# Streaming 16 experts' weights through one core's memory: one more place, single places for two more laps, one expert's gather and sums moved

## The chip, the cores and the metric

One core of a Trainium2 chip runs the whole program. The metric is device time in microseconds (us) of one execution; the time before is the median of three runs, 1548.92 us (1548.19 to 1551.0). Engines are named as in the profile: PE (TensorE) multiplies matrices, PEld is its weight load, DVE (VectorE), ACT (ScalarE) and POOL (GpSimd) work on elements, SP (SyncE) issues the loads from HBM, which 16 DMA engines carry out. The SBUF is the on-chip memory in which all tiles stand, PSUM the small one that PE writes to.

## What is computed

One encoder block on 512 tokens of 1024 numbers, in float32: an RMSNorm, a projection, two attentions (MLA with 16 heads and differential attention with 8), a gated sum with an output projection, and then a mixture of experts, which is the half that the change touches:

```
logits = h @ router_w                       # 16 experts
affinity = softmax(logits)
gate, idx = top_k(affinity per expert, 64)  # each expert picks 64 of the 512 tokens
xe = h[idx]                                 # 16 x 64 x 1024
hidden = silu(xe @ w_gate) * (xe @ w_up)    # w_gate, w_up: 16 x 1024 x 2048
ye = (hidden @ w_down) * gate               # w_down: 16 x 2048 x 1024
out = x + scatter_add(ye at idx)
```

## The kernel before

The first part, to about 600 us, is the attention and the output projection; the routing (the top 64 tokens of each expert) follows and ends at about 627 us. The rest is the experts, one after the other, and all their weights pass through the SBUF once: 402 MB.

**Chunks.** The weights are cut into 384 chunks of [128, 2048] float32, 1 MB each, 24 an expert: 8 for the gate product, 8 for the up product, 8 for the down product. PE uses them strictly in that order. In this text chunk 0 is the first one; expert 1 uses chunks 24 to 47, expert 2 chunks 48 to 71 and so on. The generator `chunks` (L719) yields a chunk at each `next(stream)` and issues its load on SP's queue; the loads stand on that queue in the order of the chunks (a manual dependency from each to the next), so a load that waits for its place holds up all behind it.

**Places.** A chunk stands in a place of 8 KB a partition, named by a letter and a number. E has 4 places, A 5 and, after the first laps, H 4 and B 6 (`REGION`, L32). In the first laps, H and B are not there yet: their memory is held by four single tiles h (the buffers that held the output projection's operand) and six single tiles b, which lie over the tiles of the output projection and the routing. Further there are two places m, one x and one c that are used at the start and then serve other tiles (m: the sums `acc`, x: the hidden layer `hh`, c: `yo`, which takes an expert's outputs).

**Laps.** `FIRST` (L34), `SECOND` (L37) and `LAP` (L41) list the places in the order in which chunks go into them, as (letter, first place, number of chunks in one load). FIRST puts 23 chunks one by one. SECOND puts 21 more chunks: m, m, A4, E one by one, A in two loads of two, then b2, h, b one by one; and then a lap of 16 chunks in loads of two over E, A, H and B. All later laps go over 16 places (4 each of E, A, H, B) in loads of four. `loads` (L702) chains the lists; the last 16 chunks are cut into loads of two and one.

When chunk 44 is used (L1016, in expert 1's down product), the tiles h and b are closed and H and B are opened over the same memory. The first load into H is a new tile over four h places, and the first into B one over all b places.

**Experts.** Two experts make a pair. `gather(pr)` (L929) picks a pair's 128 tokens: DVE makes a one-hot tile `oh` (L902) and a scaled one `ohr` (L932), PE multiplies them with the tokens `xm` (L949, 64 instructions a pair) and DVE moves the product to `xeT` (L951). Pair 0's gather runs piece by piece beside expert 0's gate product. For every later pair it runs in the middle of the pair before: after the second expert's hidden layer is transposed (L1005) and before its down product (L1011). `combine(pr)` (L907) adds a pair's outputs to the sums: the one-hot tile times the affinities, its transpose `ohT` (L914), and eight products (L920) that DVE adds to `acc` (L923). It is a generator, and one step of it is taken beside each chunk of the next expert's gate and up products (L984).

In an expert, the gate and up products are L988, the product of both is L1000, its transpose L1005, the down product L1025. `oh` and `ohr` have a pool of their own, mo2 (L683).

The code is written against a layer that places instructions on the engines' queues; `tc.issue_after(ins)` puts what is traced in its block, on the engine of `ins`, behind `ins`.

Of the kernel before, what the change touches and what calls it, by code (L numbers as in the profile page):

```python
# [11 lines left out]
F32 = mybir.dt.float32  # L12
# [9 lines left out]
T, D, NT, KT = 512, 1024, 4, 8  # L22
# [6 lines left out]
NE, CAP, FF = 16, 64, 2048  # L29


REGION = {"E": 4, "A": 5, "H": 4, "B": 6}  # L32

FIRST = [("m", 0, 1), ("m", 0, 1), ("A", 4, 1)] + [("E", i, 1) for i in range(4)] + [("x", 0, 1)]  # L34
FIRST += [("A", i, 1) for i in range(4)] + [("b", 2, 1)] + [("h", 0, 1)] * 4
FIRST += [("b", i, 1) for i in (0, 1, 3, 4, 5)] + [("c", 0, 1)]
SECOND = [("m", 0, 1), ("m", 0, 1), ("A", 4, 1)] + [("E", i, 1) for i in range(4)] + [("A", 0, 2), ("A", 2, 2)]  # L37
SECOND += [("b", 2, 1)] + [("h", 0, 1)] * 4 + [("b", i, 1) for i in (0, 1, 3, 4, 5)]

SECOND += [(r, i, 2) for r in "EAHB" for i in (0, 2)]  # L40
LAP = [(r, 0, 4) for r in "EAHB"]  # L41

LAST = 16
NPR = NE // 2
# [12 lines left out]
def build(tc, A, out):  # L57
    nc = tc.nc
    V, S, G, PE, SY = nc.vector, nc.scalar, nc.gpsimd, nc.tensor, nc.sync
# [39 lines left out]
    with ExitStack() as es:  # L99
# [60 lines left out]
        for n in range(2):  # L160
            p = ps_tile("s", "anb")
# [6 lines left out]
        for t in range(NT):  # L168
            j = p0p.tile([128, D], F32, name="junk", tag="junk", bufs=2)
# [7 lines left out]
            for n in range(2):  # L177
                xs = xt[t][:, n * 512:(n + 1) * 512]
                V.scalar_tensor_tensor(xs, xs, rx, anb[n], OP.mult, OP.mult)
                p = ps_tile("tr", "xT")  # L180
# [71 lines left out]
        r = small("r", [128, NT, 16])  # L252
# [52 lines left out]
        for t in range(NT):  # L305
            for a, (c0, c1) in enumerate(((0, 256), (256, 544))):
                p = ps_tile("pj", "zcp")[:, :c1 - c0]
                proj3(p, [h_sta(k, t) for k in range(KT)],
                      [(wc[k // 2][:, 0, k % 2, c0:c1], wc[k // 2][:, 1, k % 2, c0:c1]) for k in range(KT)])
                j = pap.tile([128, 256], F32, name="junk", tag="sq", bufs=2)  # L310
# [15 lines left out]
        for a in range(4):  # L326
            p = ps_tile("tr", "cT")
# [139 lines left out]
        for g in range(4):  # L467
            if g < 3:
                grp[g + 1] = None
            for pair in range(2):  # L470
                q, kn, kv = grp[g]
                c = 2 * g + pair
# [7 lines left out]
                p = ps_tile("tr", "rsT")  # L480
# [3 lines left out]
                p = ps_tile("pv", "pv")  # L484
# [180 lines left out]
        lap1 = ExitStack()  # L665
# [14 lines left out]
        ringE = es.enter_context(tc.tile_pool(name="ringE", bufs=1, side="right", reuse_waits="tile"))  # L680
        mo = es.enter_context(tc.tile_pool(name="moe", bufs=1, side="right", reuse_waits="tile"))
        ringA = es.enter_context(tc.tile_pool(name="ringA", bufs=1, side="right", reuse_waits="tile"))
        mo2 = es.enter_context(tc.tile_pool(name="moe2", bufs=1, side="right", reuse_waits="tile"))  # L683
        ew = A["expert_w"]
        pools = {"m": (lambda: mpool, "m8", 2), "c": (lambda: ringC, "wc", 1), "x": (lambda: ringX, "wx", 1),
                 "E": (lambda: ringE, "we", 1), "A": (lambda: ringA, "wa", 1), "B": (lambda: ringB, "wb", 1),
# [14 lines left out]

        def loads():  # L702
            todo = 3 * KT * NE
            for r, i, n in chain(FIRST, SECOND, LAP * NE * 3):
                if todo <= LAST and n == 4:
                    for j in (0, 2):
                        if todo > 2:
                            yield r, j, 2
                        else:
                            yield r, 2, 1  # L710
                            yield r, 3, 1
                        todo -= 2
                    if not todo:
                        return
                    continue
                todo -= n
                yield r, i, n
# [32 lines left out]
        for c0, c1 in ((0, 2), (2, 4), (4, 6), (6, 7), (7, 8)):  # L750
            for t in range(NT):
                hi, lo = mt_[t][:, 0, c0:c1], mt_[t][:, 1, c0:c1]
                m = mrgs[c0 // 4][:, c0 % 4:(c1 - 1) % 4 + 1, t * 128:(t + 1) * 128]
# [70 lines left out]
        for n in range(2):  # L824
# [15 lines left out]
            for t in range(NT):  # L840
                xT = wpool.tile([128, KT, 128], F32, name="xT", tag="wr", bufs=2)
                xm_part(t, 0, 4, xT, S)
                p = ps_tile("pj" if t else "s", "wo")
# [34 lines left out]
        for t in range(NT - 1):  # L878
            n = NT - 1 - t
            PE.matmul(pr_[:, :, t + 1:], on_b, mk[:, :, t, None, :].to_broadcast([128, 2, n, NE]),  # L880
                      start=False, stop=False)
        for t in range(NT):
            PE.matmul(pr_[:, 1], on_b, mk[:, 0, t, None, :].to_broadcast([128, NT, NE]),
                      start=False, stop=t == NT - 1)
# [14 lines left out]
        out_rows = out2.rearrange("t (a c) -> (t a) c", a=2)  # L899

        def one_hot(pr):
            oh = mo2.tile([128, NT, 2, CAP], F32, name="oh", tag="oh", bufs=1)  # L902
            V.tensor_tensor(oh, io[:, None, None, :].to_broadcast([128, NT, 2, CAP]),
                            slot[:, :, 2 * pr:2 * pr + 2, None].to_broadcast([128, NT, 2, CAP]), OP.is_equal)
            return oh
# [23 lines left out]
        def gather(pr):  # L929


            ohr = mo2.tile([128, NT, 2, CAP], F32, name="ohr", tag="ohr", bufs=1)  # L932
            if pr == 0:
                for t in range(NT):
                    for a in range(2):
                        V.tensor_scalar(ohr[:, t, a], io, slot[:, t, a:a + 1], rrs[:, t:t + 1],  # L936
                                        op0=OP.is_equal, op1=OP.mult)
            else:
                oh = one_hot(pr)
                V.tensor_tensor(ohr, oh, rrs[:, :, None, None].to_broadcast([128, NT, 2, CAP]), OP.mult)  # L940
            xT = mo.tile([128, KT, 128], F32, name="xeT", tag="xeT", bufs=1)
            got[pr] = xT, None, None
            n = 1 if pr == 0 else 4
            for k0 in range(0, KT, n):
                p = mps.tile([128, n, 128], F32, name="xeTp", tag="tr", bufs=2)
                for k in range(n):
                    kk = k0 + k
                    for t in range(NT):
                        PE.matmul(p[:, k], xm[:, t, kk * 128:(kk + 1) * 128],  # L949
                                  ohr[:, t].rearrange("p a s -> p (a s)"), start=t == 0, stop=t == NT - 1)  # L950
                V.tensor_tensor(xT[:, k0:k0 + n], p,  # L951
                                vT[:, FN + k0:FN + k0 + n, None].to_broadcast([128, n, 128]), OP.mult)
                yield
            if pr < NPR - 1:
                return
            sidx = mo.tile([128, 2], I32, name="sidx")
            gate = mo.tile([128, 2], F32, name="gate")
            got[pr] = xT, sidx, gate
            p = mps.tile([128, 4], F32, name="sg", tag="tr", bufs=2)
            for a in range(2):  # L960
                for hf in range(2):
                    for t in range(NT):
                        PE.matmul(p[hf * 64:(hf + 1) * 64, 2 * a:2 * a + 2], oh[:, t, a], tg[:, t, 2 * pr + a],
                                  start=t == 0, stop=t == NT - 1)
            pp = p.rearrange("p (a b) -> p a b", b=2)
            V.tensor_scalar(sidx, pp[:, :, 0], 2.0, half, op0=OP.mult, op1=OP.add)
            V.tensor_copy(gate, pp[:, :, 1])
            yield

        got = {}  # L970
        comb = iter(())
        first = gather(0)
        next(first)
        for e in range(NE):
            pr, par_ = divmod(e, 2)
            if par_ == 0:
                cur, sidx, gate = got[pr]
            gu = []
            for up in range(2):
                pp = [mps.tile([128, 512], F32, name="gu", tag="gu", bufs=5) for _ in range(2)]  # L980
                for k in range(KT):
                    if e == 0 and not up:
                        next(first, None)
                    next(comb, None)  # L984
                    wt = next(stream)
                    for j in range(2):
                        for hf in range(2):
                            PE.matmul(pp[j][hf * 64:(hf + 1) * 64], cur[:, k, par_ * 64:(par_ + 1) * 64],  # L988
                                      wt[:, hf * 1024 + j * 512:hf * 1024 + (j + 1) * 512],
                                      start=k == 0, stop=k == KT - 1)  # L990
                gu.append(pp)
                if not up:
                    if e == 0:
                        hh = ringX.tile([128, 2, 1024], F32, name="hh", tag="wx", bufs=1)
                    hid, hT = hh[:, 0], hh[:, 1].rearrange("p (k q) -> p k q", k=8)
                    for j in range(2):
                        S.activation(hid[:, j * 512:(j + 1) * 512], pp[j], AF.Silu)  # L997
# [3 lines left out]
            for j in range(2):  # L1001
                p = mps.tile([128, 512], F32, name="hTp", tag="tr", bufs=2)
# [5 lines left out]
                    S.activation(dst, p, AF.Copy)  # L1008
                else:
                    V.tensor_copy(dst, p)  # L1010
            if par_ == 1 and pr + 1 < NPR:  # L1011
                for _ in gather(pr + 1):
                    pass
            y = mps.tile([128, 512], F32, name="y", tag="y", bufs=1)
            for i in range(8):
                if e == 1 and i == 4:  # L1016
                    lap1.close()
                    ringH = es.enter_context(tc.tile_pool(name="ringH", bufs=1, reuse_waits="tile"))
                    ringB = es.enter_context(tc.tile_pool(name="ringB", bufs=1, reuse_waits="tile"))
                wt = next(stream)  # L1020
                for j in range(2):
                    kt = 2 * i + j
                    hf, f = divmod(kt, 8)
                    for a in range(2):
                        PE.matmul(y[a * 64:(a + 1) * 64], hT[:, f, hf * 64:(hf + 1) * 64],  # L1025
                                  wt[:, j, a * 512:(a + 1) * 512], start=kt == 0, stop=kt == 15)
            if pr == NPR - 1:
                ys = mo.tile([128, 512], F32, name="ys", tag="ys", bufs=1)
                V.tensor_scalar(ys, y, gate[:, par_:par_ + 1], None, op0=OP.mult)
# [44 lines left out]
```

## Time and profile before

| | us |
|---|---|
| median of three runs | 1548.92 |
| the profiled execution | 1547.91 |
| its span, first to last instruction | 1546.2 |
| PE busy | 1418.1 |
| DVE busy | 565.3 |
| ACT busy | 376.8 |
| POOL busy | 157.1 |

The span lacks 1.7 us of the execution's own time, which lie around it. PE was granted 0.979 of its full clock over the span. 441.57 MB were read from HBM, 402 of them weights of the experts. The busy times are shares of the whole; the two halves of the kernel have different limits, so the stretches of the trace are read one by one. In the trace's rows a tile's name stands before the arrow and what it is made of behind it: `wA<-in_expert_w_dram` is a load into A, `gu<-wA,xeT` a gate or up product with a chunk that stands in A. A chunk is 8 matrix instructions of PE, so x32 is four chunks.

### The profile page before, as it was taken

What the parts mean: (1) busy time and instruction counts of PE and PEld (TensorE: products, weight loads), DVE (VectorE), ACT (ScalarE), POOL (GpSimd) and SP (SyncE); (2) the same over time, 40 slices, a digit from 0 to 9 for tenths busy, and PEclk for the clock granted to TensorE, in tenths of its full rate; (3) what the DMA queues carried; (4) which work ended last, traced back from release to release, by engine and by line L of the source; (5) the groups of instructions that cost most, each with busy time, mean ns of one, the idle gap of its engine ahead of it and who ended that gap; (6) DMA issues with size and microseconds to landing.
All of it is one profiled execution on the core that took longest, in us unless ns stands there. A gap on an engine that the chain in (4) does not pass through costs nothing. (4 is left out here: it accounts for less than half of the span.)

```text
span 1546.2 us, 17925 instructions
## 1 busy us (share of the span) xinstructions
PE 1418.1 (92%) x7119; PEld 794.1 (51%) x7119; DVE 565.3 (37%) x1412; ACT 376.8 (24%) x830; POOL 157.1 (10%) x213
## 2 busy tenths in 40 slices
PE   7999999999999898799999979989989979979977
PEld 6777767788888676434334324324324324325322
DVE  8966646548888886301102102002102002102100
ACT  4545555536566643000000000000000000000000
POOL 3003213023434410000000000000000000000000
PEclk9999999999999999899999999999999999999989
DMA  4412113132222259898999999999999999999997
GB/s 158 129 53 62 58 42 105 38 92 59 76 54 54 70 193 373 306 422 370 414 433 430 432 431 431 431 433 433 432 433 433 430 432 433 432 434 432 428 421 283
DMA packets 73718, 448.50 MB, mean 290 GB/s; under 512 B 5765, under 2 KB 47809, under 8 KB 56098
## 3 DMA queue, kind: packets, MB, share of 16 engines
q1 hardware_dynamic: 72192, 444.29, 70.2%
q0 software_dynamic: 1440, 3.07, 0.8%
q8 instruction: 56, 0.92, 0.2%
q14 instruction: 28, 0.23, 0.0%
q10 hardware_dynamic: 2, 0.00, 0.0%
HBM read 441.57 MB, written 5.77 MB: 289 GB/s over the span
## 5 line engine op out<-in xcount | busy, mean ns | idle before, releaser
L1000 DVE TENSOR_TENSOR hh<-hh,gu 128x512 f32<-128x512 f32 x32 | 22.0, 688 | 428.9 <-PE gu L988 428.9
L988 PE MATMUL gu<-wA,xeT 128*64 128x512 f32 x528 | 120.7, 609 | 14.0 <-DMA wA<-in_expert_w_dram 14.0
L988 PE MATMUL gu<-wE,xeT 128*64 128x512 f32 x512 | 115.3, 601 | 11.6 <-DMA wE<-in_expert_w_dram 11.6
L988 PE MATMUL gu<-wB,xeT 128*64 128x512 f32 x448 | 103.6, 617 | 15.3 <-DMA wB<-in_expert_w_dram 15.3
L988 PE MATMUL gu<-wH,xeT 128*64 128x512 f32 x448 | 104.1, 618 | 12.4 <-DMA wH<-in_expert_w_dram 12.4
L997 ACT ACTIVATE hh<-gu 128x512 f32<-128x512 f32 x32 | 19.0, 597 | 345.6 <-PE gu L988 345.6
L211 PE MATMUL dqkv<-hl,hTh 128*128 128x384 f32 x256 | 88.4, 346 | 0.3 <-DVE hl L527 0.3
L988 PEld LDWEIGHTS gu<-wA,xeT 128*64 128x64 f32 x528 | 40.3, 140 | 91.9 <-issue 89.4
L210 PE MATMUL dqkv<-hl,hTh 128*128 128x384 f32 x256 | 87.2, 341 | 0.0
L927 POOL DMA_DIRECT2D out_dram<-acc x4 | 2.2, 558 | 824.8 <-DVE acc L923 824.8
L212 PE MATMUL dqkv<-hl,hTl 128*128 128x384 f32 x256 | 85.5, 338 | 0.0
L988 PEld LDWEIGHTS gu<-wE,xeT 128*64 128x64 f32 x512 | 36.3, 138 | 86.0 <-issue 68.2
L988 PEld LDWEIGHTS gu<-wB,xeT 128*64 128x64 f32 x448 | 32.8, 142 | 84.8 <-issue 63.9
L1008 ACT ACTIVATE hh<-hTp 128x512 f32<-128x512 f32 x16 | 9.6, 597 | 272.1 <-PE hTp L1005 272.1
L988 PEld LDWEIGHTS gu<-wH,xeT 128*64 128x64 f32 x448 | 32.1, 142 | 83.5 <-issue 64.3
L949 PEld LDWEIGHTS xeTp<-ohr,xm 128*128 128x128 f32 x512 | 59.8, 196 | 7.6 <-issue 6.3
L949 PE MATMUL xeTp<-ohr,xm 128*128 128x128 f32 x512 | 62.5, 282 | 1.3 <-DVE ohr L936 1.3
L1025 PE MATMUL y<-wH,hh 128*64 128x512 f32 x224 | 52.2, 621 | 10.9 <-DMA wH<-in_expert_w_dram 10.9
L920 PE MATMUL comb<-yo 128*128 128x512 f32 x112 | 55.5, 622 | 5.7 <-ACT yo L1037 2.8
L1038 DVE COPY yo<-y 64x512 f32<-64x512 f32 x14 | 9.7, 694 | 139.0 <-ACT yo L1037 138.9
L1025 PE MATMUL y<-wE,hh 128*64 128x512 f32 x256 | 56.5, 594 | 1.2 <-DMA wE<-in_expert_w_dram 1.2
L581 POOL TENSOR_SCALAR bias<-dist 128x512 f32<-128x512 f32 x32 | 50.0, 1569 | 48.4 <-DVE st L589 31.6
(366 smaller groups left out, 2600.0 us busy)
## 6 DMA issues: line engine op xcount, KB each, us to landing
wE<-in_expert_w_dram SPq DMA_DIRECT2D x20, 4096.0 KB, 29.1
wA<-in_expert_w_dram SPq DMA_DIRECT2D x19, 4096.0 KB, 29.7
wH<-in_expert_w_dram SPq DMA_DIRECT2D x19, 4096.0 KB, 30.1
wB<-in_expert_w_dram SPq DMA_DIRECT2D x19, 4096.0 KB, 26.5
wr<-in_w_in_dram SPq DMA_DIRECT2D x64, 192.0 KB, 2.6
wb<-in_expert_w_dram SPq DMA_DIRECT2D x12, 1024.0 KB, 12.9
wA<-in_expert_w_dram SPq DMA_DIRECT2D x6, 2048.0 KB, 13.4
wE<-in_expert_w_dram SPq DMA_DIRECT2D x9, 1024.0 KB, 7.1
```

Source lines behind the costliest of these rows:

```text
L210: PE.matmul(p, sh, mh, start=first and k == 0, stop=False)
L211: PE.matmul(p, sh, ml, start=False, stop=False)
L212: PE.matmul(p, sl, mh, start=False, stop=last and k == n - 1)
L581: G.tensor_scalar(bias, dist[:, t], slope, None, op0=OP.mult)
L920: PE.matmul(p, ohT[:, t * 128:(t + 1) * 128], ysp[:, n], start=True, stop=True)
L949: PE.matmul(p[:, k], xm[:, t, kk * 128:(kk + 1) * 128], ohr[:, t].rearrange("p a s -> p (a s)"), start=t == 0, stop=t == NT - 1)
L988: PE.matmul(pp[j][hf * 64:(hf + 1) * 64], cur[:, k, par_ * 64:(par_ + 1) * 64], wt[:, hf * 1024 + j * 512:hf * 1024 + (j + 1) * 512], star ...
L997: S.activation(hid[:, j * 512:(j + 1) * 512], pp[j], AF.Silu)
L1000: V.tensor_tensor(hs, hs, gu[1][j], OP.mult)
L1008: S.activation(dst, p, AF.Copy)
L1025: PE.matmul(y[a * 64:(a + 1) * 64], hT[:, f, hf * 64:(hf + 1) * 64], wt[:, j, a * 512:(a + 1) * 512], start=kt == 0, stop=kt == 15)
L1038: V.tensor_copy(ysp[own, 1], y[64:])
```

## The change

- There is a seventh b place, b6, and FIRST ends with it: 24 places, 24 chunks one by one. To make room, the pool mo2 goes: `oh` moves into the last 512 columns of `yo`, and `ohr` into the slot of `ys` in the pool mo.
- SECOND is replaced by MORE, 60 chunks long: a lap of 22 chunks (m, m, A4, E singly, A as 1, 2, 1, then b2, h and b singly), one of 18 (E and A in loads of two, A4, b2, h and four b singly) and one of 20 (the same with six b). Loads of four over 16 places begin with chunk 84 instead of 60.
- H and B are opened when chunk 84 is used, in the middle of expert 3's up product, instead of at chunk 44.
- The gather of pair 1 is no longer ahead of expert 1's down product but behind it. The later gathers stay where they were.
- The sums of pair 0 are no longer taken one step beside each chunk of expert 2 from its first on, but two steps beside each chunk of its up product. The later sums stay where they were.

```diff
-REGION = {"E": 4, "A": 5, "H": 4, "B": 6}
+REGION = {"E": 4, "A": 5, "H": 4, "B": 7}
...
-FIRST += [("b", i, 1) for i in (0, 1, 3, 4, 5)] + [("c", 0, 1)]
-SECOND = [("m", 0, 1), ("m", 0, 1), ("A", 4, 1)] + [("E", i, 1) for i in range(4)] + [("A", 0, 2), ("A", 2, 2)]
-SECOND += [("b", 2, 1)] + [("h", 0, 1)] * 4 + [("b", i, 1) for i in (0, 1, 3, 4, 5)]
-
-SECOND += [(r, i, 2) for r in "EAHB" for i in (0, 2)]
+FIRST += [("b", i, 1) for i in (0, 1, 3, 4, 5)] + [("c", 0, 1), ("b", 6, 1)]
+SINGLE = [("b", 2, 1)] + [("h", 0, 1)] * 4 + [("b", i, 1) for i in (0, 1, 3, 4, 5, 6)]
+MORE = [("m", 0, 1), ("m", 0, 1), ("A", 4, 1)] + [("E", i, 1) for i in range(4)]
+MORE += [("A", 0, 1), ("A", 1, 2), ("A", 3, 1)] + SINGLE
+MORE += [(r, i, 2) for r in "EA" for i in (0, 2)] + [("A", 4, 1)] + SINGLE[:-2]
+MORE += [(r, i, 2) for r in "EA" for i in (0, 2)] + [("A", 4, 1)] + SINGLE
...
-            for r, i, n in chain(FIRST, SECOND, LAP * NE * 3):
+            for r, i, n in chain(FIRST, MORE, LAP * NE * 3):
...
-            oh = mo2.tile([128, NT, 2, CAP], F32, name="oh", tag="oh", bufs=1)
+            oh = yo[:, 1536:].rearrange("p (t a s) -> p t a s", t=NT, a=2)
...
-            ohr = mo2.tile([128, NT, 2, CAP], F32, name="ohr", tag="ohr", bufs=1)
+            ohr = mo.tile([128, NT, 2, CAP], F32, name="ohr", tag="ys", bufs=1)
...
-                    next(comb, None)
+                    if e != 2:
+                        next(comb, None)
+                    elif up:
+                        with tc.issue_after(mm.ins):
+                            next(comb, None)
+                            next(comb, None)
+                    if e == 3 and up and k == 4:
+                        lap1.close()
+                        ringH = es.enter_context(tc.tile_pool(name="ringH", bufs=1, reuse_waits="tile"))
+                        ringB = es.enter_context(tc.tile_pool(name="ringB", bufs=1, reuse_waits="tile"))
...
-            if par_ == 1 and pr + 1 < NPR:
+            if par_ == 1 and 1 < pr + 1 < NPR:
                 for _ in gather(pr + 1):
                     pass
...
-                if e == 1 and i == 4:
-                    lap1.close()
-                    ringH = es.enter_context(tc.tile_pool(name="ringH", bufs=1, reuse_waits="tile"))
-                    ringB = es.enter_context(tc.tile_pool(name="ringB", bufs=1, reuse_waits="tile"))
...
+            if e == 1:
+                with tc.issue_after(mm.ins):
+                    for _ in gather(1):
+                        pass
```

In the products, `mm` is now the name of the last matrix instruction; the instructions are the same.

## Rows read from the trace of the kernel before

**Rows 1.** The page, part 2: GB/s moved in 40 slices of 38.7 us.

```profile
GB/s 158 129 53 62 58 42 105 38 92 59 76 54 54 70 193 373 306 422 370 414 433 430 432 431 431 431 433 433 432 433 433 430 432 433 432 434 432 428 421 283
```

**Rows 2.** Stretches: us, each engine busy (instructions), granted clock, DMA share, GB/s.

```profile
630.00:635.00 5.00, 5.00 (x27) 2.90 (x28) 0.87 (x3) 0.00 (x0) 0.00 (x0) 0.89 0.18 28
635.00:656.00 21.00, 21.00 (x112) 9.38 (x110) 3.44 (x8) 1.09 (x2) 0.00 (x0) 1.00 0.93 344
656.00:661.00 5.00, 5.00 (x26) 1.62 (x24) 0.00 (x0) 0.00 (x0) 0.00 (x0) 1.00 0.82 298
...
722.00:728.00 6.00, 6.00 (x32) 2.16 (x30) 2.14 (x4) 0.60 (x1) 0.00 (x0) 1.00 0.32 93
745.00:750.00 5.00, 5.00 (x20) 1.59 (x18) 1.37 (x2) 0.00 (x0) 0.00 (x0) 1.00 0.84 308
900.00:1400.00 500.00, 445.64 (x2046) 166.88 (x2042) 58.67 (x87) 22.62 (x38) 0.00 (x0) 0.98 1.00 432
...
661.00:720.00 59.00, 58.59 (x308) 25.03 (x306) 6.03 (x9) 2.98 (x5) 0.00 (x0) 1.00 1.01 427
```

**Rows 3.** Timeline of SP's queue: start us, us, engine, line, what is issued.

```profile
613.03 0.44 SPq L732 DMA_DIRECT2D wc<-in_expert_w_dram  x1
633.22 3.28 SPq L732 DMA_DIRECT2D wm<-in_expert_w_dram  x2
...
650.95 0.33 SPq L732 DMA_DIRECT2D wE<-in_expert_w_dram  x1
...
656.10 3.76 SPq L732 DMA_DIRECT2D wA<-in_expert_w_dram  x2
...
659.53 0.33 SPq L732 DMA_DIRECT2D wA<-in_expert_w_dram  x1
...
725.17 0.81 SPq L732 DMA_DIRECT2D wB<-in_expert_w_dram  x2
...
746.63 0.33 SPq L732 DMA_DIRECT2D wA<-in_expert_w_dram  x1
```

**Rows 4.** Timeline of PE in experts 0 to 3, where chunks, gather and sums stand.

```profile
652.46 7.04 PE L988 MATMUL gu<-wA,xeT 128*64 128x512 f32 x32
...
710.70 7.41 PE L949 MATMUL xeTp<-ohr,xm 128*128 128x128 f32 x64
718.04 7.09 PE L1025 MATMUL y<-wb,hh 128*64 128x512 f32 x32
...
733.42 3.03 PE L920 MATMUL comb<-yo 128*128 128x512 f32 x6 [0.69 <-ACT yo L1037]
...
742.93 3.65 PE L988 MATMUL gu<-wA,xeT 128*64 128x512 f32 x16
746.51 1.98 PE L920 MATMUL comb<-yo 128*128 128x512 f32 x4
...
798.83 7.09 PE L988 MATMUL gu<-wA,xeT 128*64 128x512 f32 x32 [0.43 <-DMA wA<-in_expert_w_dram]
808.40 8.78 PE L988 MATMUL gu<-wH,xeT 128*64 128x512 f32 x32 [2.48 <-DMA wH<-in_expert_w_dram]
```

**Rows 5.** Timeline of DVE, the last reader of the scratch tile sc.

```profile
623.83 0.28 DVE L854 MAX8 top<-sc 16x8 f32<-16x128 f32 x1
```

**Rows 6.** Loads issued at 613, 651, 656 and 660 us: KB each, us to landing.

```profile
wc<-in_expert_w_dram SPq DMA_DIRECT2D x1, 1024.0 KB, 17.3
...
wE<-in_expert_w_dram SPq DMA_DIRECT2D x1, 1024.0 KB, 5.6
...
wA<-in_expert_w_dram SPq DMA_DIRECT2D x1, 2048.0 KB, 7.3
...
wA<-in_expert_w_dram SPq DMA_DIRECT2D x1, 2048.0 KB, 8.8
```

**Rows 7.** Waits of PE for loads from 640 to 860 us: total, times, longest.

```profile
PE gu L988 <- DMA wH<-in_expert_w_dram: 2.5, 1, 2.5
...
PE gu L988 <- DMA wA<-in_expert_w_dram: 0.4, 1, 0.4
```

More of the change, by code (lines that the diff above doesn't have):

```diff
@@ L682, in build @@
         ringA = es.enter_context(tc.tile_pool(name="ringA", bufs=1, side="right", reuse_waits="tile"))
-        mo2 = es.enter_context(tc.tile_pool(name="moe2", bufs=1, side="right", reuse_waits="tile"))
         ew = A["expert_w"]
@@ L987, in build @@
                         for hf in range(2):
-                            PE.matmul(pp[j][hf * 64:(hf + 1) * 64], cur[:, k, par_ * 64:(par_ + 1) * 64],
-                                      wt[:, hf * 1024 + j * 512:hf * 1024 + (j + 1) * 512],
-                                      start=k == 0, stop=k == KT - 1)
+                            mm = PE.matmul(pp[j][hf * 64:(hf + 1) * 64], cur[:, k, par_ * 64:(par_ + 1) * 64],
+                                           wt[:, hf * 1024 + j * 512:hf * 1024 + (j + 1) * 512],
+                                           start=k == 0, stop=k == KT - 1)
                 gu.append(pp)
@@ L1024, in build @@
                     for a in range(2):
-                        PE.matmul(y[a * 64:(a + 1) * 64], hT[:, f, hf * 64:(hf + 1) * 64],
-                                  wt[:, j, a * 512:(a + 1) * 512], start=kt == 0, stop=kt == 15)
+                        mm = PE.matmul(y[a * 64:(a + 1) * 64], hT[:, f, hf * 64:(hf + 1) * 64],
+                                       wt[:, j, a * 512:(a + 1) * 512], start=kt == 0, stop=kt == 15)
+            if e == 1:
+                with tc.issue_after(mm.ins):
+                    for _ in gather(1):
+                        pass
             if pr == NPR - 1:
```

## The prediction, made before the changed kernel was run

> **What bounds the kernel now.** The kernel has two halves, and the first thing to read is the page's row of GB/s in 40 slices [rows 1]: up to slice 14 it mostly moves some tens of GB/s, from slice 21 to slice 39 it stands at 421 to 434. The second half is the 16 experts, 384 chunks of 1 MB of weights, and it runs at the speed of the loads. A view by stretches confirms it [rows 2]: from 900 to 1400 us the loads move 432 GB/s, while PE is busy 445.64 of 500 us, so 54 us of it are idle. At 432 GB/s a chunk of 1.0486 MB takes 2.43 us. Such a stage ends when the last chunk has landed, and nothing makes that earlier but time in which the loads stood still. So I read the same view where the rate is below 432, and count what each stretch lost as its length times (1 - rate/432): 4.7 us in 630 to 635 (28 GB/s), 4.3 in 635 to 656 (344), 1.6 in 656 to 661 (298), 0.7 in 661 to 720 (427), 4.7 in 722 to 728 (93), 1.4 in 745 to 750 (308). That is 17 us, and PE is busy through all of these: here the loads wait for places that PE still reads.
>
> The queue's rows say which place each hole waits for [rows 3]. All 23 places are asked for by 613.03; the next load, into the first m, goes out only at 633.22, when PE has used chunk 0. Up to 651 the loads then follow PE at 2.95 us a chunk (two issues of 0.33 span 3.28), since PE does a piece of the first gather beside each chunk. At 656.10 a load of two chunks into A goes out, which needs chunks 8 and 9. At 725.17 the first load into B goes out. It brings two chunks and needs only b0 and b1 for that, but it begins a new tile over all six b places, and 725.17 is the end of chunk 43 (b5), the last of the four that PE does from 718.04 [rows 4]. At 746.63 the first load of four into A goes out, as chunk 51 ends (742.93 + 3.65). Both places come back late because they come back in blocks, and PE has just done 7.41 us of gather (710.70) and does 8.0 us of sums in three pieces (3.03, 3.03, 1.98) from 733.42 on [rows 4].
>
> **The 24th place** (the last entry of FIRST). Place b6 lies over the scratch tile sc of the routing, whose last reader ends at 624.1 [rows 5]. The load of chunk 23 can go out then, behind the load into c (613.03, landing 17.3 us later [rows 6], 630.3), and lands at about 632.7, in time in which nothing moved. The m load still waits for 633.22, but brings chunk 24 instead of 23: from there on every place brings a later chunk. Worth one chunk, 2.4 us; nothing, if b6 comes free only after 633.
>
> **A in pieces of 1, 2 and 1** (MORE). PE does the four A chunks from 652.46 at 1.72 us each (7.04 less an overlap of some 0.17, over 4) [rows 4], so A0 is free at 654.4 and not, with A1, at 656.1. The load before it is issued at 650.95 and lands 5.6 us later [rows 3, 6], at 656.6, so the engines then hardly run empty. A1 and A2 follow at 657.8; a load of two that met an empty queue took 7.3 us [rows 6], which gives 665.1, and three chunks at 2.43 after 656.6 give 663.9. I take 665.0 for chunk 33, near the slower end. Before, chunk 33 landed at 659.53 + 8.8 = 668.3 [rows 3, 6]. By here 3.3 us are gained, 2.4 by the 24th place and 0.9 by this piece (between 0 and the 1.6 that 656 to 661 lost).
>
> **Singles and pairs up to chunk 84** take the two block waits away. Before, the block of chunks 80 to 83 landed at 798.8, where PE's wait for it ends [rows 4]. From chunk 33 that is 130.5 us for 50 chunks, where 50 x 2.427 is 121.4: 9.1 lost. 6.1 of it are the holes at 722 and 745, the rest the slow start after each. In return 34 of the 50 chunks come singly, at the 427 GB/s of 661 to 720, where most loads are singles [rows 2]: 2.456 us each, 34 x 0.03 = 1.0. Chunk 83 lands at 665.0 + 121.4 + 1.0 = 787.4, 11.4 us earlier.
>
> **Does a new wait come instead?** I follow PE through the new order with the old durations [rows 4]. Expert 1 ends its up half as before; its down half starts where the gather started, 710.70, and takes 8 x 1.72, to 724.5. The gather follows to 731.9, the gate half of expert 2 to 745.6, its up half with 8.0 us of sums and 0.7 of transposes to 768. The loads of chunks 64 and 65 need chunks 46 and 47 (724.5) and are wanted when chunk 63 is about to land, 665 + 30 x 2.45 = 738.5. Chunks 66 and 67 need 49 (735.4), wanted at 743.4. 70 and 71 need 53 (742.3), wanted at 753. The first block of four, 84 to 87, needs 67 (about 777), wanted at 787. The block into B now needs all seven b places, the last with chunk 83 (about 804), and brings 96 to 99, wanted at 816. Everywhere 8 us or more are left; a load wants about 1 of them between issue and first byte.
>
> **The gather and the sums behind.** Their PE time is the same, 7.41 and 8.0 us, only later. Were neither moved, chunk 49 would end at 740.0, where the first two thirds of expert 2's sums are still ahead [rows 4], and chunk 53 at some 752, against wanted times of 743 and 753. So for the loads I cost the moves at nothing; they give margin. What covers them on PE is the stock of loaded chunks: from 640 to 860 PE waits for loads 0.4 and 2.5 us [rows 7]. The gather's evacuation now stands directly ahead of the gate half, but only its second part, under 1 us, and four steps of the gate half cover that. The one-hot tile moves into the free end of yo and ohr into the slot of ys; both had one buffer and have one. SP issues some 20 more loads of 0.33 us on a queue that mostly waits. Nothing, each; if a cover is gone, it comes out of the 8 us of margin.
>
> **The sum** is 3.3 + 9.1 - 1.0 = 11.4 us. All later loads shift by as much: from 900 us on there is no hole to absorb it, and PE, with 54 idle us in 500, can follow. The profiled execution took 1547.91 us (its span is 1546.2), which would become 1536.5. The median of the runs is 1.0 higher, 1548.92, so I forecast 1537.5.
>
> **Rivals.** *Part of it is lost*: b6 comes free late (2.4 less, 1540), or PE reaches expert 2 later than I count, so that a hole stays (4 to 6 less, 1541.5 to 1543.5). For it: a margin of 8 us is no more than one gather. Against it: every duration is from the row of the same instruction. 19 in 100.
>
> *Slower: the single loads run one at a time.* From 635 to 656 us singles go out 2.95 us apart and move 344 GB/s, 3.05 us a chunk [rows 2, 3]. That happens when each place comes free less than one transfer ahead. If it held for the 24 chunks that are newly single (44 and 45, ten of 54 to 63, twelve of 72 to 83), they would cost 24 x (3.05 - 2.43) = 14.9 us, more than what is gained: 1548.9 - 12.4 + 14.9 = 1551.4 (12.4 is the sum without its 1.0 for singles). It decides from 20 such chunks on. The Trainium skill, page "DMA: Bandwidth & Descriptors", section "Bandwidth", speaks for this one: it has 341 GB/s for a load of 1 MB by itself and 425 for 16 MB, and advises large loads; by its figures the 24 chunks would cost an estimated 24 x 0.61 = 14.6 us. The trace agrees with that from 635 to 656, where loads come alone. Against it: from 661 to 720 singles are queued ahead of the engines, and 427 GB/s are moved; by the margins above the new ones are queued ahead as well. 6 in 100.
>
> *No change*: with 16 places from chunk 84 on, the loads wait later for what they gained early, and it ends at 1549. That needs PE to fall 16 chunks behind in experts 4 and 5; its idle time speaks against it. 6 in 100.
>
> **How the numbers follow.** My own case has 69 in 100: 1535 to 1540, with 0 to 2.4 for the 24th place, 0 to 1.6 for the A piece and 6.1 to 9.1 for the block waits. The range of 1534.5 to 1543.0 takes in most of the partial case and leaves out some 15 in 100. About 0.2%, 3 us, is what a measurement of this kernel can tell from no change. Faster by more than that, below 1545.8, are my case and the partial one, 0.88. The same 0.06, slower 0.06.
>
> **What would show it.** In the profile after: a load into b6 at about 624, and nothing moving for some 1.7 us before 634 instead of 4; a load into A at 654.4; no stretch under 420 GB/s from 665 to 900; in expert 1 the down half and then the gather, and the sums in the up half of expert 2; the first block of four landing near 797, where PE now waits for its chunks until 808.4 [rows 4]. I am wrong if the rate shows a hole between 730 and 860, if singles queued ahead move under 400 GB/s, or if the holes are gone and the end is not earlier by the same time.

## Result and profile after

The changed kernel takes 1538.76 us (median of four runs, 1537.32 to 1539.41), beside 1548.99 us for the kernel before (1548.19 to 1551.0): a ratio of 0.9931, with a 95% interval of 0.9914 to 0.9948. That is 10.2 us, where 11.4 were forecast. The profiled execution took 1537.32 us, its span is 1535.6. All medians here are of executions at the usual clock: one slow execution of the kernel with 23 places (1606.57 us, granted clock 0.846) and one of the kernel before (1791.11 us, 0.748) are left out.

The page's row of GB/s in 40 slices (here of 38.4 us) answers to [rows 1]. In the kernel before, slices 17 to 20 read 306, 422, 370 and 414; now they read 345, 404, 428 and 428:

```profile
GB/s 159 129 54 63 58 43 105 38 90 63 75 50 59 65 196 355 345 404 428 428 432 434 434 431 431 435 431 432 431 432 434 431 432 436 427 432 435 428 421 278
```

The stretches of the changed kernel (us, busy time of PE, PEld, DVE, ACT and POOL with instructions, granted clock, DMA share, GB/s) answer to [rows 2]:

```profile
629.00:634.00 5.00, 5.00 (x24) 2.18 (x25) 0.58 (x2) 0.00 (x0) 0.00 (x0) 0.82 0.24 59
634.00:655.00 21.00, 21.00 (x112) 9.35 (x110) 1.46 (x5) 1.09 (x2) 0.00 (x0) 1.00 0.96 348
655.00:660.00 5.00, 5.00 (x26) 1.71 (x24) 0.00 (x0) 0.00 (x0) 0.00 (x0) 1.00 0.92 333
660.00:665.00 5.00, 5.00 (x26) 1.45 (x22) 0.56 (x1) 0.00 (x0) 0.00 (x0) 1.00 0.98 418
665.00:720.00 55.00, 54.59 (x260) 19.68 (x260) 6.86 (x11) 2.98 (x5) 0.00 (x0) 1.00 1.01 428
720.00:740.00 20.00, 20.00 (x126) 11.53 (x124) 2.08 (x3) 0.59 (x1) 0.00 (x0) 1.00 1.02 432
740.00:760.00 20.00, 20.00 (x76) 6.37 (x72) 7.25 (x11) 1.77 (x3) 0.00 (x0) 1.00 1.00 423
760.00:900.00 140.00, 135.53 (x644) 50.49 (x644) 18.32 (x28) 6.54 (x11) 0.00 (x0) 1.00 1.01 433
900.00:1400.00 500.00, 447.77 (x2100) 173.31 (x2097) 61.25 (x91) 23.22 (x39) 0.00 (x0) 0.98 1.00 432
```

The holes at 722 and 745 (93 and 308 GB/s before) are gone: 432 and 423. The stretch beside the first gather, 634 to 655, moves what it moved before (348 GB/s, 344 before). Ahead of the first m load there is still a hole. The same eight microseconds of both kernels, the kernel before first, then the changed one:

```profile
628.00:636.00 8.00, 8.00 (x40) 5.05 (x39) 2.32 (x8) 0.00 (x0) 0.00 (x0) 0.81 0.32 105
...
628.00:636.00 8.00, 8.00 (x41) 4.25 (x40) 0.88 (x3) 0.00 (x0) 0.00 (x0) 0.82 0.52 191
```

That is 8 x (1 - 105/432) = 6.1 us lost before and 4.5 after. The prediction's sign was 4 and then 1.7: both sizes were too small by 2 us or more. The hole is shorter by 1.6 us: a chunk, 2.4 us, less the 0.8 by which the m load of this execution came later after the load into c (632.04 - 611.05 = 20.99 us, where it was 633.22 - 613.03 = 20.19 [rows 3]).

The timeline of SP's queue in the changed kernel (start us, us, engine, line, operation), which answers to [rows 3]:

```profile
611.05 0.44 SPq L733 DMA_DIRECT2D wc<-in_expert_w_dram  x1
622.16 0.33 SPq L733 DMA_DIRECT2D wb<-in_expert_w_dram  x1
632.04 3.28 SPq L733 DMA_DIRECT2D wm<-in_expert_w_dram  x2
...
653.21 0.33 SPq L733 DMA_DIRECT2D wA<-in_expert_w_dram  x1
...
656.64 0.33 SPq L733 DMA_DIRECT2D wA<-in_expert_w_dram  x1
```

And that of PE at the end of expert 1, which answers to the second part of [rows 4]:

```profile
709.57 10.52 PE L1031 MATMUL y<-wb,hh 128*64 128x512 f32 x48
...
723.46 7.41 PE L950 MATMUL xeTp<-ohr,xm 128*128 128x128 f32 x64
730.80 3.65 PE L998 MATMUL gu<-wE,xeT 128*64 128x512 f32 x16
```

The load into b6 goes out at 622.16, right as the last reader of sc ends, the load into A0 at 653.21 by itself (the one into A1 and A2 follows at 656.64), and the gather stands behind the down product. All of this is as the prediction drew it, only some 1.2 us earlier: the first m is reloaded at 632.04, not 633.22.

**A yardstick for all runs.** That shift belongs to the first half of the program, which the runs hardly touch (it gains the load into b6) and which ends at another moment in each execution: the first m load went out between 632.04 and 636.16 us over the profiles of this study. From there on the loads set the pace. So I compare the runs by the span less the start of that load, and call it the second half. Each is read from one profile. It was 1546.2 - 633.22 = 913.0 us before and 1535.6 - 632.04 = 903.6 us after, 9.4 less. A second profile of the changed kernel, with a load at 635.09 and a span of 1538.5, has 903.4.

### The profile page after: what moved, and what is told of

Its sections match the earlier page's. It is cut to its first block, busy times and chain, and to the rows that moved or that the text cites. A ratio compares the mean times of both kernels' runs of the same rounds, so it can differ in the third digit from the quotient of the medians.

```text
span 1535.6 us, 17967 instructions
## 1 busy us (share of the span) xinstructions
PE 1414.2 (92%) x7119; PEld 792.8 (52%) x7119; DVE 564.6 (37%) x1412; ACT 376.9 (25%) x830; POOL 156.7 (10%) x213
## 5 line engine op out<-in xcount | busy, mean ns | idle before, releaser
L998 PE MATMUL gu<-wA,xeT 128*64 128x512 f32 x512 | 114.9, 601 | 9.8 <-DMA wA<-in_expert_w_dram 9.8
L998 PE MATMUL gu<-wH,xeT 128*64 128x512 f32 x384 | 86.4, 604 | 14.7 <-DMA wH<-in_expert_w_dram 14.7
L998 PE MATMUL gu<-wB,xeT 128*64 128x512 f32 x384 | 88.1, 613 | 11.6 <-DMA wB<-in_expert_w_dram 11.6
L998 PEld LDWEIGHTS gu<-wA,xeT 128*64 128x64 f32 x512 | 36.6, 138 | 85.3 <-issue 70.1
L998 PEld LDWEIGHTS gu<-wB,xeT 128*64 128x64 f32 x384 | 29.4, 141 | 69.5 <-issue 66.3
L998 PEld LDWEIGHTS gu<-wH,xeT 128*64 128x64 f32 x384 | 27.4, 139 | 72.7 <-issue 52.4
L1031 PE MATMUL y<-wA,hh 128*64 128x512 f32 x256 | 57.1, 595 | 1.2 <-DMA wA<-in_expert_w_dram 1.2
L1047 ACT ACTIVATE yo<-y 64x512 f32<-64x512 f32 x14 | 8.2, 589 | 196.8 <-PE y L1031 196.8
```

Source lines behind the costliest of these rows:

```text
L998: mm = PE.matmul(pp[j][hf * 64:(hf + 1) * 64], cur[:, k, par_ * 64:(par_ + 1) * 64], wt[:, hf * 1024 + j * 512:hf * 1024 + (j + 1) * 512], ...
L1031: mm = PE.matmul(y[a * 64:(a + 1) * 64], hT[:, f, hf * 64:(hf + 1) * 64], wt[:, j, a * 512:(a + 1) * 512], start=kt == 0, stop=kt == 15)
L1047: S.activation(ysp[own, 0], y[:64], AF.Copy)
```

## The experiments

Ten runs were made, nine kernels and the changed one once more. The table has for each the median of its runs, the ratio to the kernel before, run on the same chip, with its 95% interval, and the second half of its profile.

| kernel | median us | ratio [interval] | first m load, span | second half |
|---|---|---|---|---|
| before | 1548.99 | 1 | 633.22, 1546.2 | 913.0 |
| changed | 1538.76 | 0.9931 [0.9914, 0.9948] | 632.04, 1535.6 | 903.6 |
| changed, again | 1538.99 | 0.9937 [0.9923, 0.9950] | 635.09, 1538.5 | 903.4 |
| both moves alone | 1543.70 | 0.9962 [0.9949, 0.9975] | 636.16, 1544.5 | 908.3 |
| gather's move alone | 1545.68 | 0.9983 [0.9974, 0.9993] | 633.31, 1543.9 | 910.6 |
| sums' move alone | 1546.16 | 0.9982 [0.9973, 0.9991] | 634.28, 1545.5 | 911.2 |
| 24th place alone | 1549.10 | 0.9999 [0.9991, 1.0008] | 634.77, 1548.1 | 913.3 |
| changed, moves undone | 1539.76 | 0.9936 [0.9923, 0.9949] | 635.15, 1538.4 | 903.3 |
| changed, 23 places | 1540.40 | 0.9947 [0.9932, 0.9962] | 633.09, 1539.3 | 906.2 |
| changed, 120 more singles | 1543.65 | 0.9966 [0.9953, 0.9978] | 634.16, 1541.9 | 907.7 |
| gate and up in turn | 1536.80 | 0.9924 [0.9910, 0.9939] | 632.82, 1535.0 | 902.2 |
| the same, A singly | 1536.53 | 0.9925 [0.9911, 0.9938] | 632.13, 1534.0 | 901.9 |

### The changed kernel with both moves undone

```diff
-                    if e != 2:
-                        next(comb, None)
-                    elif up:
-                        with tc.issue_after(mm.ins):
-                            next(comb, None)
-                            next(comb, None)
+                    next(comb, None)
...
-            if par_ == 1 and 1 < pr + 1 < NPR:
+            if par_ == 1 and pr + 1 < NPR:
...
-            if e == 1:
-                with tc.issue_after(mm.ins):
-                    for _ in gather(1):
-                        pass
```

Expected:

> The changed kernel with both moves taken back: 24 places, single places to chunk 84, gather and sums where they were. The prediction: the moves are only margin, no hole opens, 1538 to 1540 us (changed kernel: 1538.8). Its tightest places are the loads into A2 and A3 that need chunk 53, with 0.3 us left. Rival: the margins are too thin, holes of 2 to 5 us open between 740 and 755, 1541 to 1544.

Measured: 1539.76 us, and a second half of 903.3, that of the changed kernel. Its stretches where a hole was to be feared:

```profile
720.00:740.00 20.00, 20.00 (x90) 6.71 (x89) 4.85 (x7) 1.19 (x2) 0.00 (x0) 1.00 1.02 429
740.00:760.00 20.00, 20.00 (x79) 6.32 (x80) 4.82 (x7) 1.19 (x2) 0.00 (x0) 1.00 1.00 425
```

No hole opens, though PE does gather and sums as early as it did before. In the changed kernel the two moves are margin that nothing uses, as the prediction had it; the places alone do it.

### The two moves without the places

The edit is the same one the other way round, on the kernel before.

> The kernel before with the two moves alone (pair 1's gather behind expert 1's down product, pair 0's sums in expert 2's up half); 23 places and the block laps as before. Theory A, the block waits are set by when PE ends chunk 43 and chunk 51: with the gather behind, chunk 43 ends near 717.7 us and not at 725.2, five us before chunk 55 has landed, and chunk 51 near 739 and not at 746.6. Both holes vanish without any new place or lap, and the time is 1540 to 1543 us (6 to 9 earlier than 1549). Theory B, as the prediction has it: the moves are worth nothing to the loads, 1548 to 1550.

Measured: 1543.70 us, 4.7 us off the second half (913.0 to 908.3). The moves by themselves do close the holes. PE's timeline at the end of chunk 43 and SP's queue there:

```profile
720.58 7.07 PE L1030 MATMUL y<-wE,hh 128*64 128x512 f32 x32
```

```profile
720.81 0.81 SPq L732 DMA_DIRECT2D wB<-in_expert_w_dram  x2
...
742.04 0.33 SPq L732 DMA_DIRECT2D wA<-in_expert_w_dram  x1
```

And its stretches (the last two columns are DMA share and GB/s):

```profile
720.00:730.00 10.00, 10.00 (x57) 5.19 (x54) 0.69 (x1) 0.59 (x1) 0.00 (x0) 1.00 1.01 434
740.00:750.00 10.00, 10.00 (x50) 3.48 (x48) 0.51 (x1) 1.68 (x3) 0.00 (x0) 1.00 0.98 406
750.00:800.00 50.00, 49.80 (x214) 16.47 (x212) 10.44 (x16) 1.34 (x4) 0.00 (x0) 1.00 1.00 424
```

The load into B goes out at 720.81, as chunk 43 ends and the next down chunks begin (720.58): 84.7 us after this run's first m load (636.16), where it was 91.95 before. No stretch stands still: 434 GB/s where the first hole was. What is left are small losses, 406 and 424. So theory A was right that the moves close the holes, and its time was 0.7 us too good at its slow end. Theory B, taken from a sentence of the prediction that was meant for the new laps, is wrong for the old ones: with blocks, the moves are worth about 5 us, with single places nothing. They are two cures for one illness.

### Each move alone

```diff
-            if par_ == 1 and pr + 1 < NPR:
+            if par_ == 1 and 1 < pr + 1 < NPR:
                 for _ in gather(pr + 1):
                     pass
...
+            if e == 1:
+                with tc.issue_after(mm.ins):
+                    for _ in gather(1):
+                        pass
```

> The kernel before with pair 1's gather behind expert 1's down product, nothing else. Theory: the hole ahead of the first load into B goes (chunk 43 ends near 717.7 instead of 725.2), but the load into A that needs chunk 51 still starts near 746.6, since gather and sums now stand together ahead of it; the second hole grows by what the first gave back, 6 to 7 us instead of 1, and the time is 1548 to 1549.5. Rival: each hole is worth its own time, and closing the first gains 4 to 5 us, 1543.5 to 1544.5.

Measured: 1545.68 us, 2.4 us off the second half. Neither of the two: the first hole closes, as both said, and the second grows, but not by all of it. SP's queue, and then the stretches:

```profile
717.96 0.81 SPq L732 DMA_DIRECT2D wB<-in_expert_w_dram  x2
...
742.35 0.33 SPq L732 DMA_DIRECT2D wA<-in_expert_w_dram  x1
```

```profile
738.00:744.00 6.00, 6.00 (x24) 1.64 (x22) 1.53 (x3) 0.00 (x0) 0.00 (x0) 1.00 0.76 279
751.00:757.00 6.00, 6.00 (x22) 1.94 (x22) 2.06 (x3) 1.19 (x2) 0.00 (x0) 1.00 0.82 309
```

The load into A goes out at 742.35, not near 746.6. The expectation took PE's order over from the kernel before, where 8.0 us of sums stand in three pieces beside the first chunks of expert 2 [rows 4]. With the gather in the gap, PE's order has one sum beside each chunk, and so only two pieces of 1.12 us stand ahead of chunk 51 (the row at 740.37), where two of 3.03 did before:

```profile
736.39 1.12 PE L920 MATMUL comb<-yo 128*128 128x512 f32 x2
737.45 1.94 PE L988 MATMUL gu<-wA,xeT 128*64 128x512 f32 x8
739.32 1.12 PE L920 MATMUL comb<-yo 128*128 128x512 f32 x2
740.37 1.94 PE L988 MATMUL gu<-wA,xeT 128*64 128x512 f32 x8
```

So the hole at 738 to 744 loses 6 x (1 - 279/432) = 2.1 us and a third one, at 751 to 757, 1.7.

The sums alone moved:

> The kernel before with pair 0's sums in expert 2's up half, nothing else. The first hole stays as it was (chunk 43 near 725.2). Theory: chunk 51 ends near 739, before the loads of chunks 60 to 63 are done, so the second hole closes for its own 2 to 3 us: 1545.5 to 1547. Rival: it moves to the next block, and nothing is gained, 1548 to 1549.5.

Measured: 1546.16 us, 1.8 us off the second half. The hole ahead of B stays, the one ahead of A closes, for its own price. The stretch at the first hole, and SP's queue:

```profile
720.00:730.00 10.00, 10.00 (x50) 3.42 (x48) 0.00 (x0) 0.00 (x0) 0.00 (x0) 1.00 0.54 202
```

```profile
726.24 0.81 SPq L732 DMA_DIRECT2D wB<-in_expert_w_dram  x2
...
739.97 0.33 SPq L732 DMA_DIRECT2D wA<-in_expert_w_dram  x1
```

### The 24th place alone

Blocks as before, gather and sums as before; b6 ends FIRST, and the second lap leaves out a b place, so that the blocks begin at chunks 44 and 60 again.

```diff
-REGION = {"E": 4, "A": 5, "H": 4, "B": 6}
+REGION = {"E": 4, "A": 5, "H": 4, "B": 7}
...
-SECOND = [("m", 0, 1), ("m", 0, 1), ("A", 4, 1)] + [("E", i, 1) for i in range(4)] + [("A", 0, 2), ("A", 2, 2)]
-SECOND += [("b", 2, 1)] + [("h", 0, 1)] * 4 + [("b", i, 1) for i in (0, 1, 3, 4, 5)]
+MORE = [("m", 0, 1), ("m", 0, 1), ("A", 4, 1)] + [("E", i, 1) for i in range(4)]
+MORE += [("A", 0, 1), ("A", 1, 2), ("A", 3, 1)] + SINGLE[:-2]
+MORE += [(r, i, 2) for r in "EAHB" for i in (0, 2)]
...
```

(The moves of `oh` and `ohr` to other tiles are in this kernel too.)

> The 24th place and the A pieces of 1, 2 and 1 alone, with gather and sums where they were, blocks of two from chunk 44 and of four from chunk 60 (one b place fewer in the second lap, so that the blocks begin at the same chunks as before). If the terms of the prediction stand by themselves, it gains their 3.3 us, 1545.6. Rival: the load into B still starts when PE ends the last b chunk, near 725, whatever came before it; the hole ahead of it grows by what was gained, and the time is that of the kernel before, 1548.5 to 1549.5.

Measured: 1549.10 us, a ratio of 0.9999 (0.9991 to 1.0008). The rival's time is right, and the term does not stand by itself. SP's queue, and the stretch in which the gain is lost:

```profile
625.58 0.33 SPq L732 DMA_DIRECT2D wb<-in_expert_w_dram  x1
634.77 3.28 SPq L732 DMA_DIRECT2D wm<-in_expert_w_dram  x2
...
691.95 3.76 SPq L732 DMA_DIRECT2D wE<-in_expert_w_dram  x2
...
726.73 0.80 SPq L732 DMA_DIRECT2D wB<-in_expert_w_dram  x2
...
748.18 0.33 SPq L732 DMA_DIRECT2D wA<-in_expert_w_dram  x1
```

```profile
690.00:695.00 5.00, 5.00 (x26) 1.72 (x24) 0.00 (x0) 0.00 (x0) 0.00 (x0) 1.00 0.55 174
```

The chunk is loaded in the idle time, at 625.58. But the load into B goes out 726.73 - 634.77 = 92.0 us after the first m load, as it did before (725.17 - 633.22 = 91.95 [rows 3]), and the one into A 113.4 after it, as before. PE's pace sets both. The rival had the hole ahead of B grow; it did not. What was gained at 630 is given back before it, in a hole of its own: from 690 to 695 only 174 GB/s are moved, 5 x (1 - 174/432) = 3.0 us, where the kernel before moved 433 and the second lap of this kernel, which leaves out a b place, makes its first load of two into E (691.95) wait for chunk 28. A lap that keeps the place was not run; that the load into B would still wait there for the last b chunk is argued, not shown.

### The changed kernel with 23 places

```diff
-FIRST += [("b", i, 1) for i in (0, 1, 3, 4, 5)] + [("c", 0, 1), ("b", 6, 1)]
+FIRST += [("b", i, 1) for i in (0, 1, 3, 4, 5)] + [("c", 0, 1)]
...
-MORE += [("A", 0, 1), ("A", 1, 2), ("A", 3, 1)] + SINGLE
-MORE += [(r, i, 2) for r in "EA" for i in (0, 2)] + [("A", 4, 1)] + SINGLE[:-2]
-MORE += [(r, i, 2) for r in "EA" for i in (0, 2)] + [("A", 4, 1)] + SINGLE
+MORE += [("A", 0, 2), ("A", 2, 2)] + SINGLE
+MORE += [(r, i, 2) for r in "EA" for i in (0, 2)] + [("A", 4, 1)] + SINGLE[:-1]
+MORE += [(r, i, 2) for r in "EA" for i in (0, 2)] + [("A", 4, 1)] + SINGLE[:-1]
```

(SINGLE ends with b5 here; blocks of four begin with chunk 80, and H and B are opened there.)

> The changed kernel without its 24th place: b6 is never loaded, A is loaded as 2 and 2, two single laps of 18, blocks of four from chunk 80. With no hole behind to hide it, the whole term of the prediction is lost: 2.4 to 3.3 us, 1541.2 to 1542.1. Rival: the 24th place gave less, since the loads still stood still for 2.3 us ahead of the m load; then 1539.5 to 1540.5.

Measured: 1540.40 us, in the rival's range, and a second half of 906.2, 2.6 to 2.8 longer than the changed kernel's (903.6 and 903.4), in the range of the first. Here, with no hole behind to swallow it, the 24th place with its A piece is worth 2.6 to 2.8 us by the second halves and 1.4 to 1.6 by the medians, of the 3.3 in the sum.

### 120 more chunks singly

The lap of 20 stands eleven times, up to chunk 284, and H and B are opened there. So 120 more chunks come singly and 80 more in loads of two, all of which came in loads of four.

```diff
-MORE += [(r, i, 2) for r in "EA" for i in (0, 2)] + [("A", 4, 1)] + SINGLE
+MORE += ([(r, i, 2) for r in "EA" for i in (0, 2)] + [("A", 4, 1)] + SINGLE) * 11
```

> The changed kernel with its lap of 20 (4 loads of two, 12 of one) repeated up to chunk 284, so that 120 more chunks come singly. By the prediction's price (427 against 432 GB/s, 0.03 us a single) it is 3 to 4 us slower than the changed kernel, 1541.5 to 1543. By the rival (344 GB/s, 0.62 us a single) it is some 74 us slower, about 1613.

Measured: 1543.65 us, 4.9 us more than the changed kernel's first median and just above the first range; the second half is 4.1 to 4.3 longer. That is 0.034 to 0.041 us a single, with the loads of two counted in. Where 12 of 20 chunks come singly the loads move 428 GB/s, where the changed kernel moved 432. Its stretch from 900 to 1100:

```profile
900.00:1100.00 200.00, 183.03 (x854) 67.95 (x852) 29.29 (x43) 9.55 (x17) 0.00 (x0) 1.00 1.01 428
```

The rival that singles run one at a time is out: it asked for 0.62 each. By the Trainium skill's table on the page "DMA: Bandwidth & Descriptors", section "Bandwidth", the estimate was 0.61. This run differs from it by a factor of 15 or more.

### A version that beats both

What is left after the change is the stretch beside the first gather, 348 GB/s from 634 to 655: PE does a gather step beside each gate chunk of expert 0 and gives a place back every 2.95 us. If gate and up chunks come in turn, a step stands beside two chunks.

```diff
                 src = ew[e, q, :, j * FF:(j + n) * FF]
+                if c < 16:
+                    src = ew[0, 2 * (c % 2) + c // 8, :, c // 2 % 4 * FF:(c // 2 % 4 + 1) * FF]
...
+            if e == 0:
+                both = [[mps.tile([128, 512], F32, name="gu", tag="gu", bufs=5) for _ in range(2)] for _ in range(2)]
+                for k in range(KT):
+                    next(first, None)
+                    for up in range(2):
+                        wt = next(stream)
...
```

> The changed kernel with expert 0's gate and up chunks in turn (gate step 0, up step 0, gate step 1 ...), so that a step of the first gather stands beside two chunks instead of one. PE then gives a place back every 2.3 us on the mean instead of every 2.95 from the first m load on, about as fast as a load takes (2.43), and reaches chunk 8 near 4 x 1.2 us earlier. Theory: the loads from 632 to 654 close up, 3.5 to 5 us less than the changed kernel, 1534 to 1535.5. Rival: PE has no stock to gain from and the loads wait later for what they gained, 1538 to 1539.5.

Measured: 1536.80 us, 2.0 below the changed kernel's first median, and a second half 1.2 to 1.4 shorter. That is less than the theory had. The queue and the stretches show where it stays:

```profile
639.21 7.96 SPq L735 DMA_DIRECT2D wE<-in_expert_w_dram  x4
651.51 6.72 SPq L735 DMA_DIRECT2D wA<-in_expert_w_dram  x3
```

```profile
648.00:652.00 4.00, 4.00 (x24) 1.88 (x22) 0.29 (x1) 0.00 (x0) 0.00 (x0) 1.00 1.01 420
652.00:656.00 4.00, 4.00 (x24) 1.77 (x22) 0.29 (x1) 0.00 (x0) 0.00 (x0) 1.00 0.88 313
656.00:660.00 4.00, 4.00 (x24) 1.86 (x22) 0.29 (x1) 0.00 (x0) 0.00 (x0) 1.00 0.82 289
```

From 648 to 652 the loads have closed up, to 420 GB/s; from 652 on they lose again. Two things fit this, and only the second was tried: chunk 7's place, x, takes no new chunk, so that the loads into E3 (646.84, the last of the four) and A0 (651.51) go out 4.67 us apart, and A1 with A2 waits for one more gather step. So the next run split that pair, `[("A", i, 1) for i in range(4)]`:

> Expert 0's gate and up chunks in turn, as in the run before, and the second lap's A1 and A2 in loads of their own instead of one of two. There the load of two went out near 656.2, when PE had done the gather step between chunks 9 and 10, and the loads moved 313 and 289 GB/s from 652 to 660. Theory: A1 can go out 2.9 us earlier, the hole closes, and it takes 1.5 to 2.5 us less than with the pair, 1534.3 to 1535.3. Rival: the hole is that of place x, which takes no further chunk, and nothing changes, 1536.5 to 1537.

Measured: 1536.53 us, a second half of 901.9, 0.3 shorter. The rival is right on the time: splitting the pair closes little of the hole. That x is what keeps the rest open was not tried. The same stretches:

```profile
652.00:656.00 4.00, 4.00 (x24) 1.88 (x22) 0.29 (x1) 0.00 (x0) 0.00 (x0) 1.00 0.96 291
656.00:660.00 4.00, 4.00 (x24) 1.79 (x22) 0.29 (x1) 0.00 (x0) 0.00 (x0) 1.00 0.94 375
```

Beside it the changed kernel ran once more.

> The changed kernel itself, beside the run above: 1538 to 1539.5. Measured from its reload of the first m, the last chunk should land 893 us later, as in its first profile, whenever the first half ends.

Measured: 1538.99 us, as expected. So the best version is 2.5 us below it on the same chip (1535.7 to 1537.79 against 1537.45 to 1540.23 over five runs each), of which the second halves show 1.5.

## Why the prediction was right, and where its sizes were off

The direction, the mechanism and the range held: 1538.76 lies between 1534.5 and 1543.0, 1.3 us above the forecast of 1537.5. In part that nearness is luck: the medians are 10.2 us apart, the second halves 9.4, and the change hardly touches the first half. By the second halves the 11.4 of the sum were 2.0 too many.

Two rows of the changed kernel are used below, of the loads of chunk 34 (into A3, issued at 658.36 us) and of chunk 83 (into b6, issued at 768.38). The last number is the time to landing, so they landed at 666.4 and 787.8:

```profile
wA<-in_expert_w_dram SPq DMA_DIRECT2D x1, 1024.0 KB, 8.0
...
wb<-in_expert_w_dram SPq DMA_DIRECT2D x1, 1024.0 KB, 19.4
```

- *The loads bound the second half, and only their idle time counts.* Shown: from 900 to 1400 us the changed kernel moves 432 GB/s as before, so nothing absorbs what was gained by 800, and it is in the time. PE follows: it is busy 447.77 of these 500 us.
- *The two block waits go* (9.1 less 1.0 for singles). Both holes are gone, but this is the term that was sized too large. In the changed kernel chunk 34 lands at 666.4 and chunk 83 at 787.8 (the rows above), so 49 chunks take 121.4 us, 2.478 each. For 50 chunks that is an estimated 123.9, where the sum had 122.4 and the kernel before took 130.5: 6.6 us gained, not 8.1. The kernel with 23 places agrees, 913.0 - 906.2 = 6.8. The 9.1 was the whole slack between two landings, and 3 us of that, beyond the 6.1 of the holes, were called the slow start after each and taken as gained. Most of those were not there to gain. A single's 0.034 to 0.041 us, where 0.03 was put, makes 0.1 to 0.4 of the difference, and the 423 GB/s from 740 to 760 another 20 x (1 - 423/432) = 0.4; where the rest stays, no row shows.
- *The 24th place and the A piece* (3.3). Right in place, time and size by the landings: chunk 34 at 666.4 puts chunk 33 at some 664.0, 31.9 us after the first m load, where the sum had 665.0 - 633.22 = 31.8 and the kernel before 668.3 - 633.22 = 35.1. Of the 3.2 us, 2.6 to 2.8 are left in the second half, as the run with 23 places shows. What the prediction did not say is that this term depends on the other: alone, it is worth nothing.
- *No new wait*. Right: no stretch shown from 665 to 900 is below 420 (cut into pieces of 5 us, two read 408 and 410), and the block of chunks 84 to 87, forecast for 797, was issued at 776.07 (forecast: about 777) and landed 21.5 us later, at 797.6. The landing is not as good as it looks, since this execution's first half ended 1.2 us early.
- *The moves at nothing*. Right for the changed kernel, as its run without them shows. That they close the same holes by themselves was not seen.
- *The slower rival* and *no change* are out by the runs above. The reading that the slower one rests on was wrong as well: from 635 to 656 the loads do not come alone. They go out 2.95 us apart and one of them takes 5.6 us to land [rows 3, 6], so two are under way at a time, and PE's pace of a place in 2.95 us allows no more than 1.0486 MB / 2.95 us = 355 GB/s. With gate and up chunks in turn, where places come back faster, the same single loads moved 420 from 648 to 652. That 344 lies near 341 is no evidence for a price of single loads. The *partial* one, a b6 that comes free late or a hole that stays, did not come either.

## What to carry to other kernels

When a stage runs at the speed of its loads, list the holes in time order with what ends each: a wait for a fixed point of another engine swallows everything that is gained ahead of it, so the last hole must go first, and a gain measured alone may read zero. Here, places that are given back one by one needed no reordering of the work around them; with blocks, the reordering alone brought half of what the whole change brings (4.7 of 9.4 us). And a first half that ends at another moment in each execution hides 1 us effects: measure from the event where the stage that you changed begins.

## What was not expected

- The first half, nearly the same in all kernels, let the first m load go between 632.04 and 636.16 us, 4.1 us apart, while the second half of the changed kernel repeated within 0.2 us (903.6 and 903.4).
- Moving the gather alone changed the order of other instructions too: the sums' pieces of 3.03 us fell apart into steps of 1.12 beside each chunk.
- A load of 1 MB that is queued ahead costs only 0.034 to 0.041 us more than its share of a load of 4 MB.
